# Side work placed between the pieces of a step, and a softmax handed out in stages, in a streaming attention layer

## The chip, the cores and the metric

The kernel runs on one core of one Trainium2 chip. The metric is the device time of one execution in microseconds. The profile is of one further execution on the same kind of core.

## What is computed

One layer of an encoder with two token mixers side by side, for one new stream of 2048 frames and for eight running streams of 16 frames with a past of 512. Cut to what matters here:

```
h = adaln(x, c);  qa, ka, va, za, qb, kb, vb, zb, ga, gb = split(h @ w_in)     # A and B, 512 wide each
# A, differential attention, 4 heads of 2 x 64
p = softmax(mask(qa . ka / 8));  oa = (p[first] - lam * p[second]) @ va
# B, stick-breaking attention, 8 heads of 64
log_a = log_sigmoid(z) + reverse_cumsum(log_sigmoid(-z)) - log_sigmoid(-z);  ob = exp(log_a) @ vb
# merge
y = (sigmoid(ga) * ((rms(oa) * silu(za)) @ w_branch_a) + sigmoid(gb) * ((ob * silu(zb)) @ w_branch_b)) @ w_out
```

The outputs are the normed streams and the new keys and values of both mixers.

## The kernel before

**Number format.** Every float32 operand of a large product is split into two float16 halves, a high and a low one, and a product is three matmuls. A split needs a power of two as its scale, and that comes from the sum of the squares of the operand. So each weight and each cached key or value is loaded (SyncE's queue), squared and summed on ScalarE (`sum_squares`, L282 in the profile), its sum is spread over the partitions by a small matmul (`total`, L221), and it is then split (`split`: the high half on ScalarE, L300, or on GpSimd, L302, the low half on VectorE, L305).

**Units and steps.** The main part of the kernel goes through eight units; even ones are a head of A, odd ones two heads of B. A unit has 17 steps: the tile of the sampled streams (`t == NT`, no scores here) and 16 tiles of 128 frames. A step of tile `t` computes the scores of that tile against all earlier keys in chunks of 512 (`scores`, L660 and L661, the mask L664), and takes some pieces of the projections, which run about five steps ahead on a line of their own (L446; the gate's, in B units, L522; the transposes L535 and L539).

**A's softmax.** The chunk's scores are copied out of their bank by VectorE with a running maximum (L576). After a tile's last chunk `softmax_pair` takes the maximum (L607), four exponentials on ScalarE for a tile of two segments (L124), the sums (L617 to L620), a join of the two softmaxes for each segment (L624), and then `turn`: the split into halves (L300, L305) and a transposing DMA into `wt` (L598).

**B's weights.** ScalarE takes two sigmoids of a chunk (L124), VectorE scans one of them straight out of the bank (L637), GpSimd multiplies (L643), and `turn` splits (L590, L591) and transposes.

**The products with the values.** `turn` puts the matmuls of a segment (L717 to L719 in A, L721 and L722 in B) on the list `due`, to be given out when `spent`, a count of the microseconds of TensorE's work that the text has given out, has grown by `PV_LAG`. `give` runs the pieces of a step in order, adds their cost to `spent`, and gives out what is due.

**Side work.** While unit u is at work, `prepare_unit(u + 1)` makes a list of pieces: loads of the next unit's weights with the squares one piece behind, the scale (`bounds`), the splittings (`cut`, `gate_cut`). Two further lists are `spare` (loads and squares of the last weights and of the cached values, L878) and `cached` (cached keys: load, square, then splitting and storing, L898 to L901). At the beginning of each step the loop takes some pieces off these lists and runs them, before the step's scores and projections:

```
for fn in back[: -(-len(back) // max(1, (W_READY if u else W_READY + 2) - t % NT))]:
    back.pop(0)()
```

**Order.** The program text gives each instruction a place; from it a scheduler with a model of the chip sets the order on each engine when the kernel is built. An instruction whose inputs the model takes as ready may be put ahead of others that stand before it in the text. `act` is a helper that chains ScalarE's table functions, so that these keep the order of the text; `sum_squares` does not use it. Raw buffers come from the list `free` and go back to it, so how early a load can be issued depends on the buffers. The bank tags are `mm` (2), `s` (3, the scores), `t` (1) and `o` (2).

**The end.** After the units, a last part multiplies with the branch weights and the output weights, and does the sampled streams' attention beside it (from about 1830 us on). The first part (to about 143 us) makes `h`.

Of the kernel before, what the change touches and what calls it, by code (L numbers as in the profile page):

```python
# [4 lines left out]


# [14 lines left out]
AF = mybir.ActivationFunctionType  # L21
# [4 lines left out]
P = 128  # L26
# [12 lines left out]
SEG = 8  # L39
PV_LAG = 30.0  # L40
PIECE, CHUNK, PV_A, PV_B = 0.44, 0.22, 0.17, 0.085
# [73 lines left out]
def layer_kernel(ctx: ExitStack, tc: tile.TileContext, a: dict):  # L115
# [160 lines left out]

    def sum_squares(src, n, dst, width=1024, scale=1.0):

        for i in range(0, n, width):
            junk = tiny.tile([P, width], F16, tag="junk", name="junk", bufs=1)  # L280
            w = min(width, n - i)
            S.activation(out=junk[:, 0:w], in_=src[:, i : i + w], func=AF.Square, scale=scale,  # L282
                         accum_out=dst[:, i // width : i // width + 1])

# [32 lines left out]
    def prepare_unit(u, keep=None):  # L317
# [30 lines left out]

# [234 lines left out]
    def turn(job, seg, scale=None):  # L583
# [15 lines left out]
        if job["t"] < NT:  # L599
            cost = (PV_A, PV_B)[job["U"]["kind"]]  # L600
            due.extend((spent[0] + PV_LAG, cost, fn) for fn in pv(job, seg))

    def softmax_pair(job):

        segs = job["segs"]
        nm = tiny.tile([P, 2], F32, tag="nm", name="nm")
        V.tensor_reduce(out=nm, in_=job["mx"][:, :, 0 : job["nch"]], axis=AX.X, op=ALU.max, negate=True)  # L607
        l = tiny.tile([P, 2, 2], F32, tag="l", name="l")
        for i, seg in enumerate(segs):
            nk = (seg["hi"] - seg["lo"]) * P  # L610
            for c in range(2):
                w = seg[("p", "n")[c]][:, 0:nk]
                act(out=w, in_=w, func=AF.Exp, bias=nm[:, c : c + 1], accum_out=l[:, c, i : i + 1])
        r = tiny.tile([P, 3], F32, tag="r", name="r")
        sums = l[:, :, 0]
        if len(segs) > 1:
            V.tensor_tensor(out=sums, in0=l[:, :, 0], in1=l[:, :, 1], op=ALU.add)  # L617
        V.reciprocal(out=r[:, 0:2], in_=sums)
        V.scalar_tensor_tensor(out=r[:, 2:3], in0=sums[:, 0:1], scalar=r[:, 1:2], in1=nlam, op0=ALU.mult, op1=ALU.mult)
        V.tensor_tensor(out=r[:, 0:1], in0=r[:, 0:1], in1=ls[:, 0:1], op=ALU.mult)  # L620
        for seg in segs:
            nk = (seg["hi"] - seg["lo"]) * P
            p, n = seg["p"][:, 0:nk], seg["n"][:, 0:nk]
            V.scalar_tensor_tensor(out=p, in0=n, scalar=r[:, 2:3], in1=p, op0=ALU.mult, op1=ALU.add)  # L624
            turn(job, seg, r[:, 0:1])

# [96 lines left out]

    due, spent = [], [0.0]

# [17 lines left out]
    def give(order, costs):  # L743

        for i, weight, fn in order:
            fn()
            spent[0] += weight * costs[i]
            while due and due[0][0] <= spent[0]:
                _, cost, product = due.pop(0)
                product()  # L750
                spent[0] += cost
# [109 lines left out]
    def norms():  # L861
# [124 lines left out]
    with tc.tile_pool(name="p0", bufs=1) as p0:  # L986
# [156 lines left out]
        interleave(normed(0))  # L1143
        for fn in early[0:5]:
            fn()
# [57 lines left out]
        interleave(modulated(4))  # L1203
        interleave([(1.0, fn) for fn in early[5:]], modulated(0), normed(1))
        free.extend(first_x)
# [119 lines left out]
    for n in range(len(steps) + 2):  # L1325
        made, qk = [], []
        if n < len(steps):
# [17 lines left out]
        if at[0] == len(line) and not pieces and not spare and not cached:  # L1345
# [4 lines left out]
            if n == len(steps) + 1:  # L1350
                pieces += [(PV_B / PIECE, fn) for _, _, fn in due]
                due.clear()
        give(interleaved(pieces, qk), (PIECE, CHUNK))
    c01.close()
# [158 lines left out]
```

## Time and profile before

| | us |
|---|---|
| median of three runs | 2300.79 |
| lowest, highest | 2296.86, 2304.49 |
| the profiled execution | 2304.59 |
| its span, first to last instruction | 2302.8 |
| mean granted TensorE clock | 0.969 |

The page of the profile gives each engine's busy time and share, and the costliest groups of instructions. The views by stretch give the busy time of each engine in a window of the span. In the lists of waits, a line "PE ps_s L660 <- DVE sc_n L637: 33.7, 38, 2.8" says that TensorE's matmuls of line 660 stood idle for 33.7 us in 38 waits, the longest 2.8, until an instruction of line 637 on VectorE was done. Names such as `sc_n` are the program's tiles: `sc_p` and `sc_n` hold scores, `wt` the transposed weights, `ps_...` are banks, `junk` is where the squares are thrown away, `wa` and `wb` are the buffers of the list `free`.

### The profile page before, as it was taken

The page shows a single profiled execution, that of the slowest core. Times are in us where ns is not written, and L with a number is a line of the kernel's source. Part 1 is how long each engine was busy: PE and PEld are TensorE (multiplying, and loading weights), DVE is VectorE, ACT ScalarE, POOL GpSimd, SP SyncE. Part 2 cuts the span into 40 slices and gives each one's busy share as a digit, 9 for nine tenths or more (in the row PEclk, how much of TensorE's full clock was granted, in tenths as well). Part 3 has the DMA queues.
Part 4 walks back from the last instruction along what each step waited for, and adds up shares of the span by engine and source line. Part 5 has one row for each costly group of instructions (what it writes and reads, how often), then busy time and mean ns, then how long its engine had stood idle before and what let it go on. Part 6 is the DMA issues. An engine that isn't in the chain of part 4 may idle for free. (4 is left out here: it accounts for less than half of the span.)

```text
span 2302.8 us, 41756 instructions
## 1 busy us (share of the span) xinstructions
PE 2098.3 (91%) x14752; PEld 1130.4 (49%) x14752; DVE 1724.1 (75%) x3795; ACT 1622.1 (70%) x3228; POOL 697.6 (30%) x610
## 2 busy tenths in 40 slices
PE   5999998988999999889998988999998688999998
PEld 3655554544555445455554544555454344444443
DVE  4668776779875877998676769976778877777663
ACT  4978776878876776887677788866677666566551
POOL 1232033456311433743033346401334311111211
PEclk8999999999999999999999999999998898999999
DMA  9778778888895898789779699774777899889431
GB/s 328 267 240 213 159 169 213 179 197 188 197 235 143 225 211 196 169 177 266 162 193 229 149 223 197 179 171 120 158 157 158 177 276 248 219 218 239 140 107 47
DMA packets 805827, 445.30 MB, mean 193 GB/s; under 512 B 537354, under 2 KB 744506, under 8 KB 805104
## 3 DMA queue, kind: packets, MB, share of 16 engines
q1 hardware_dynamic: 804668, 442.24, 78.3%
q8 instruction: 115, 1.88, 0.3%
q14 instruction: 96, 0.79, 0.1%
q10 hardware_dynamic: 948, 0.39, 0.1%
HBM read 228.82 MB, written 86.02 MB: 137 GB/s over the span
## 5 line engine op out<-in xcount | busy, mean ns | idle before, releaser
L643 POOL TENSOR_TENSOR sc_p<-sc_p,sc_n 128x127 f32<-128x127 f32 (+7 forms) x192 | 314.5, 1640 | 744.7 <-DVE sc_n L637 505.3
L446 PEld LDWEIGHTS <-hs 128*128 128x128 f16 x3120 | 293.7, 99 | 312.6 <-issue 7.9
L446 PE MATMUL ps_mm<-wb,hs 128*128 128x512 f16 x1734 | 433.8, 382 | 0.0
L446 PE MATMUL ps_mm<-wa,hs 128*128 128x512 f16 x1386 | 338.9, 380 | 1.9 <-DVE v L305 1.9
L637 DVE TENSOR_TENSOR_SCAN sc_n<-ps_s,sc_n,zero_t 128x512 f32<-128x512 f32 x192 | 245.6, 1279 | 67.3 <-ACT ps_s L124 62.8
L660 PE MATMUL ps_s<-k,qst 128*128 128x512 f16 (+3 forms) x640 | 225.4, 353 | 61.5 <-DVE sc_n L637 45.7
L522 PEld LDWEIGHTS <-hs 128*128 128x128 f16 x1632 | 156.3, 99 | 188.5 <-DVE qst L550 12.2
L591 DVE TENSOR_TENSOR sc_n<-sc_p,sc_n 128x128 f16<-128x128 f32 (+7 forms) x192 | 213.4, 1116 | 41.0 <-ACT sc_n L590 40.4
L124 ACT ACTIVATE sc_p<-ps_s,usc 128x512 f32<-128x512 f32 (+3 forms) x320 | 203.9, 637 | 41.1 <-PE ps_s L661 23.9
L661 PE MATMUL ps_s<-k,qst 128*128 128x512 f16 (+3 forms) x640 | 226.1, 354 | 0.0
L522 PE MATMUL ps_t<-wb,hs 128*128 128x512 f16 x918 | 218.8, 379 | 1.9 <-DVE qst L550 1.9
L124 ACT ACTIVATE ps_s<-ps_s,usc 128x512 f32<-128x512 f32 (+3 forms) x328 | 199.1, 607 | 0.0
L590 ACT CAST sc_n<-sc_p 128x128 f16<-128x128 f32 (+7 forms) x192 | 154.5, 808 | 62.7 <-POOL sc_p L643 62.0
L1427 PE MATMUL ps_o<-wo,wa 128*128 128x512 f16 x816 | 184.7, 382 | 0.7 <-ACT wa L1240 0.7
L522 PE MATMUL ps_t<-wa,hs 128*128 128x512 f16 x714 | 172.9, 384 | 8.1 <-DVE qst L550 4.7
L721 PE MATMUL ps_o<-v,wt 128*128 128x128 f16 x1088 | 132.4, 225 | 25.3 <-DMA wt<-sc_n 25.2
L576 DVE TENSOR_SCALAR_CACHE_REDUCE sc_p<-ps_s,usc 128x512 f32<-128x512 f32 (+3 forms) x160 | 106.2, 663 | 43.8 <-PE ps_s L661 28.4
L487 POOL TENSOR_TENSOR rot<-pr,rope 128x256 f32<-128x256 f32 x68 | 60.5, 889 | 245.9 <-ACT pr L460 202.8
L721 PEld LDWEIGHTS <-wt 128*128 128x128 f16 x1088 | 102.0, 102 | 55.0 <-DMA wt<-sc_n 31.8
L637 DVE TENSOR_TENSOR_SCAN sc_n<-ps_s,zero_t 128x128 f32<-128x128 f32 (+3 forms) x128 | 104.2, 814 | 32.0 <-ACT ps_s L124 31.3
L1427 PEld LDWEIGHTS <-wa 128*128 128x128 f16 x816 | 78.6, 98 | 95.3 <-issue 2.6
L722 PE MATMUL ps_o<-v,wt 128*128 128x64 f16 x1088 | 123.7, 197 | 0.0
(369 smaller groups left out, 4520.9 us busy)
## 6 DMA issues: line engine op xcount, KB each, us to landing
hs<-hT_d SPq DMA_DIRECT2D x130, 512.0 KB, 4.1
g_d<-gt SPq DMA_DIRECT2D x68, 256.0 KB, 5.3
wb<-g_d SPq DMA_DIRECT2D x34, 512.0 KB, 4.7
out_dram<-pr SPq DMA_DIRECT2D x204, 64.0 KB, 2.0
wa<-in_w_in_dram SPq DMA_DIRECT2D x34, 256.0 KB, 4.7
o_d<-o SPq DMA_DIRECT2D x136, 64.0 KB, 2.8
hs<-o_d SPq DMA_DIRECT2D x17, 512.0 KB, 7.1
out_dram<-x SPq DMA_DIRECT2D x17, 512.0 KB, 2.8
```

Source lines behind the costliest of these rows:

```text
L124: i = S.activation(**kw)
L446: T.matmul(box["p"], box["h"][:, hi, k, :], U["w"][k][:, wi, :], start=(n == 0), stop=(n == 3 * KT - 1))
L522: T.matmul(box["g"][:, 0:gw], box["h"][:, hi, k, :], U["wg"][k // per][:, k % per, wi, :], start=(j == 0), stop=(j == 3 * KT - 1))
L590: S.copy(out=hi, in_=src)
L591: V.tensor_tensor(out=lo, in0=src, in1=hi, op=ALU.subtract)
L637: V.tensor_tensor_scan(out=dst[:, lo : lo + n][:, ::-1], data0=src[:, 0:n][:, ::-1], data1=zero_t[:, 0:1].to_broadcast([P, n]), initial=fi ...
L643: G.tensor_tensor(out=p[:, 0:m], in0=p[:, 0:m], in1=n[:, 1 : m + 1], op=ALU.mult)
L660: T.matmul(p[:, 0:n], qst[:, c, :], kk[:, c, 0:n], start=True, stop=False)
L661: T.matmul(p[:, 0:n], qst[:, 2 + c, :], kk[:, c, 0:n], start=False, stop=not diag)
L721: T.matmul(po[:, c * P : (c + 1) * P], wt[:, wj, :], vt[:, c, :, :], start=first, stop=False)
L722: T.matmul(po[:, c * P : c * P + 64], wt[:, nb + wj, :], vt[:, c, 0, :], start=False, stop=last)
L1427: T.matmul(po, st["y"][:, yi * 8 + k, :], wo[j * 4 + k // 2][:, wi, k % 2, :], start=(n == 0), stop=(n == 3 * KT - 1))
```

## The change

1. `sum_squares` gets `keep`. With it, the square is pinned behind the instruction that stands before it in the text on ScalarE. It is set for the preparation of units 1 to 7, for `spare` and for `cached`.
2. In a preparation, a square stands two pieces behind its load, where it stood one behind. So each list of loads has one piece more, and the first stage runs six early pieces of unit 0 instead of five.
3. The pieces of `back`, `spare` and `cached`, and unit 7's branch weight, are collected in `side` and interleaved with the step's projections and chunks, at no cost in `spent`.
4. `softmax_pair` no longer issues everything at once. It puts stages on the list `due`, by work given out since the tile's last chunk: the exponentials at 1.0, the sums at 3.0 plus two for each full segment (`n_all` is the tile's length in segments of eight blocks), the join of segment i at that plus i, and its `turn` 1.5 later. The sampled tile's is still issued at once.
5. `PV_LAG` is 27 instead of 30; it counts from `turn`. The list `due` is now kept in order of due time.

```diff
-PV_LAG = 30.0
+PV_LAG = 27.0
+TURN_LAG = 1.5
+EXP_LAG = 1.0
+SUM_LAG = 2.0
...
-    def sum_squares(src, n, dst, width=1024, scale=1.0):
+    def sum_squares(src, n, dst, width=1024, scale=1.0, keep=False):
...
+            x = S.activation(out=junk[:, 0:w], in_=src[:, i : i + w], func=AF.Square, scale=scale,
+                             accum_out=dst[:, i // width : i // width + 1])
+            if keep:
+                tc.keep_in_program_order(x)
...
-            sum_squares(raw[name, k], 1024, U[name + "acc"][:, i : i + 1])
+            sum_squares(raw[name, k], 1024, U[name + "acc"][:, i : i + 1], keep=u > 0)
...
-                if i > 0:
-                    norm(name, ks[i - 1], i - 1)
-            return [lambda i=i: piece(i) for i in range(len(ks) + 1)]
+                if i > 1:
+                    norm(name, ks[i - 2], i - 2)
+            return [lambda i=i: piece(i) for i in range(len(ks) + 2)]
...
-            due.extend((spent[0] + PV_LAG, cost, fn) for fn in pv(job, seg))
+            for fn in pv(job, seg):
+                later_on(PV_LAG, fn, cost)
...
+        stages = [(EXP_LAG, lambda i=i, c=c: powers(i, c)) for i in range(len(segs)) for c in range(2)]
+        stages.append((EXP_LAG + SUM_LAG + 2.0 * n_all, sums))
+        for i, seg in enumerate(segs):
+            at = EXP_LAG + SUM_LAG + 2.0 * n_all + i
+            stages += [(at, lambda seg=seg: joined(seg)), (at + TURN_LAG, lambda seg=seg: turn(job, seg, r[:, 0:1]))]
+        for lag, fn in stages:
+            if job["t"] == NT:
+                fn()
+            else:
+                later_on(lag, fn)
...
+    def later_on(lag, fn, cost=0.0):
+
+        spent[1] += 1
+        bisect.insort(due, (spent[0] + lag, spent[1], cost, fn))
...
-                sum_squares(st, 1024, dst, scale=scale)
+                sum_squares(st, 1024, dst, scale=scale, keep=True)
...
-            sum_squares(fetched[0][0], 1024, acc)
+            sum_squares(fetched[0][0], 1024, acc, keep=True)
...
-        for fn in early[0:5]:
+        for fn in early[0:6]:
...
             if u == 7 and not back and not spare and not cached and len(branch_weights) > 1:
-                branch_weight()
+                side.append((1.0, branch_weight))
             for fn in back[: -(-len(back) // max(1, (W_READY if u else W_READY + 2) - t % NT))]:
-                back.pop(0)()
+                side.append((1.0, back.pop(0)))
...
-                        todo.pop(0)()
+                        side.append((1.0, todo.pop(0)))
...
-        give(interleaved(pieces, qk), (PIECE, CHUNK))
+        give(interleaved(pieces, qk, side), (PIECE, CHUNK, 0.0))
```

`powers`, `sums` and `joined` hold the same instructions as before, in functions of their own.

More of the change, by code (lines that the diff above doesn't have):

```diff
@@ L7 @@
+import bisect
 import math
@@ L281, in sum_squares @@
             w = min(width, n - i)
-            S.activation(out=junk[:, 0:w], in_=src[:, i : i + w], func=AF.Square, scale=scale,
-                         accum_out=dst[:, i // width : i // width + 1])
+            x = S.activation(out=junk[:, 0:w], in_=src[:, i : i + w], func=AF.Square, scale=scale,
+                             accum_out=dst[:, i // width : i // width + 1])
+            if keep:
+                tc.keep_in_program_order(x)
     def add_up(acc, n):
@@ L608, in softmax_pair, with powers, sums, joined @@
         l = tiny.tile([P, 2, 2], F32, tag="l", name="l")
[L609 to L613, printed above, removed]
-        r = tiny.tile([P, 3], F32, tag="r", name="r")
[L615 to L621, printed above, removed]
+        r = tiny.tile([P, 3], F32, tag="r", name="r")
+        n_all = sum(seg["hi"] - seg["lo"] for seg in segs) / SEG
+        def powers(i, c):
+            seg = segs[i]
+            w = seg[("p", "n")[c]][:, 0 : (seg["hi"] - seg["lo"]) * P]
+            act(out=w, in_=w, func=AF.Exp, bias=nm[:, c : c + 1], accum_out=l[:, c, i : i + 1])
+        def sums():
+            sums = l[:, :, 0]
+            if len(segs) > 1:
+                V.tensor_tensor(out=sums, in0=l[:, :, 0], in1=l[:, :, 1], op=ALU.add)
+            V.reciprocal(out=r[:, 0:2], in_=sums)
+            V.scalar_tensor_tensor(out=r[:, 2:3], in0=sums[:, 0:1], scalar=r[:, 1:2], in1=nlam, op0=ALU.mult, op1=ALU.mult)
+            V.tensor_tensor(out=r[:, 0:1], in0=r[:, 0:1], in1=ls[:, 0:1], op=ALU.mult)
+        def joined(seg):
             nk = (seg["hi"] - seg["lo"]) * P
@@ L722, in pv_block @@
             T.matmul(po[:, c * P : c * P + 64], wt[:, nb + wj, :], vt[:, c, 0, :], start=False, stop=last)
-    due, spent = [], [0.0]
+    due, spent = [], [0.0, 0]
+    def later_on(lag, fn, cost=0.0):
+        spent[1] += 1
+        bisect.insort(due, (spent[0] + lag, spent[1], cost, fn))
     def pv(job, seg):
@@ L748, in give @@
             while due and due[0][0] <= spent[0]:
-                _, cost, product = due.pop(0)
+                _, _, cost, product = due.pop(0)
                 product()
@@ L1203, in layer_kernel @@
         interleave(modulated(4))
-        interleave([(1.0, fn) for fn in early[5:]], modulated(0), normed(1))
+        interleave([(1.0, fn) for fn in early[6:]], modulated(0), normed(1))
         free.extend(first_x)
@@ L1325, in layer_kernel @@
     for n in range(len(steps) + 2):
-        made, qk = [], []
+        made, qk, side = [], [], []
         if n < len(steps):
@@ L1350, in layer_kernel @@
             if n == len(steps) + 1:
-                pieces += [(PV_B / PIECE, fn) for _, _, fn in due]
+                while due and due[0][2] == 0.0:
+                    due.pop(0)[3]()
+                pieces += [(PV_B / PIECE, fn) for _, _, _, fn in due]
                 due.clear()
-        give(interleaved(pieces, qk), (PIECE, CHUNK))
+        give(interleaved(pieces, qk, side), (PIECE, CHUNK, 0.0))
+    for _, _, _, fn in due:
+        fn()
     c01.close()
```

1 line of the change is left out of this document (removed).

## The prediction

> **What bounds the kernel now.** I read the page first, then the busy time of each engine by stretch, then TensorE's own waits, then who waits in the line that sums squares, and last a stretch of the timeline.
>
> ```profile
> PE 2098.3 (91%) x14752; PEld 1130.4 (49%) x14752; DVE 1724.1 (75%) x3795; ACT 1622.1 (70%) x3228; POOL 697.6 (30%) x610
> ```
>
> TensorE is busy for 91% of the span and no other engine for more than 75%, so the time is TensorE's work plus its idle time. The next view gives, for stretches cut where the score work changes kind, the length and then the busy microseconds of PE, PEld, DVE, ACT and POOL, and after them the granted clock. In order they are the units 0 (A), 1 (B), 2 (A), 3 (B), 4 (A), 5 (B), 6 (A), and 7 (B) up to where its projections run out.
>
> ```profile
> 143.00:298.00 155.00, 149.79 (x1059) 83.33 (x1057) 124.72 (x351) 123.15 (x279) 27.64 (x29) 0.99 0.78 197
> 298.00:548.00 250.00, 231.66 (x1595) 122.76 (x1593) 194.26 (x322) 193.34 (x399) 113.12 (x89) 0.98 0.84 193
> 548.00:728.00 180.00, 167.69 (x1155) 93.30 (x1155) 139.33 (x384) 134.27 (x302) 40.68 (x45) 0.97 0.83 191
> 728.00:979.00 251.00, 230.88 (x1643) 124.90 (x1641) 198.24 (x333) 194.13 (x399) 112.50 (x91) 0.99 0.87 200
> 979.00:1157.00 178.00, 166.65 (x1164) 93.03 (x1163) 140.38 (x388) 135.42 (x304) 40.68 (x45) 0.98 0.83 196
> 1157.00:1415.00 258.00, 234.66 (x1635) 125.61 (x1633) 195.84 (x328) 196.89 (x407) 113.69 (x93) 0.97 0.88 202
> 1415.00:1586.00 171.00, 162.04 (x1152) 89.25 (x1152) 138.67 (x380) 122.22 (x279) 41.65 (x42) 1.00 0.69 162
> 1586.00:1755.00 169.00, 165.51 (x1161) 88.76 (x1160) 134.57 (x226) 121.29 (x256) 63.40 (x50) 1.00 0.70 158
> ```
>
> Unit 7 is the control that this kernel carries in itself. It does the same score work as units 1, 3 and 5, with VectorE as busy (134.57 of 169, 80%, against 198.24 of 251, 79%), but it has next to no side work, and TensorE is busy for 97.9% of it, against 92.7, 92.0 and 91.0% in units 1, 3 and 5. So side work costs TensorE time where it stands now, and VectorE's load alone does not. At unit 7's share, units 1, 3 and 5 would last 236.6, 235.8 and 239.7 us, which is 46.9 less; at unit 0's share (96.6%), units 2, 4 and 6 would last 173.6, 172.5 and 167.7, 15.2 less. These 62 us bound what a better order of side work can give.
>
> What TensorE waits for between 143 and 1755 us (total, times, longest), and below it the same for unit 1 and for the control:
>
> ```profile
> PE ps_s L660 <- DVE sc_n L637: 33.7, 38, 2.8
> PE ps_o L717 <- DMA wt<-sc_n: 14.7, 10, 3.8
> PE ps_s L660 <- DVE sc_n L576: 9.1, 7, 3.3
> PE ps_o L721 <- DMA wt<-sc_n: 7.2, 6, 2.3
> ...
> PE ps_s L660 <- DVE sc_n L637: 9.9, 10, 2.8
> ...
> PE ps_s L660 <- DVE sc_n L637: 1.5, 1, 1.5
> ```
>
> The first row is a score matmul without a free bank, since the scan that empties the bank is late. Units 3 and 5 show the same 9.9 as unit 1; the control shows 1.5 in 169 us.
>
> Why the scan is late is seen at the line that sums squares, where ScalarE sits idle until a load lands:
>
> ```profile
> L282 ACT ACTIVATE junk<-wa x64: 1038/1057/1112, 250.4 to 1463.1; 128x1024 f16<-128x1024 f32 x64
> ...
>   DMA wa<-in_cache_a_k_dram: 14.4, 9
>   DMA wb<-in_w_in_dram: 14.2, 10
>   DMA wa<-in_w_in_dram: 13.0, 6
>   DMA wa<-in_cache_b_k_dram: 10.9, 7
>   DMA wb<-in_cache_b_k_dram: 7.2, 4
>   DMA wb<-in_cache_b_v_dram: 6.3, 2
>   DMA wa<-in_cache_a_v_dram: 6.0, 3
> ```
>
> These seven rows are 72.0 us of ScalarE standing still for squares in 41 waits. None of it is in the control, as the last of these squares starts at 1463.1. One of them in the timeline (start, length, engine and line; in brackets the idle time before and what ended it):
>
> ```profile
> 812.61 0.40 SPq L878 DMA_DIRECT2D wa<-in_cache_a_v_dram  x1
> ...
> 818.55 1.06 ACT L282 ACTIVATE junk<-wa 128x1024 f16<-128x1024 f32 x1 [3.93 <-DMA wa<-in_cache_a_v_dram]
> ...
> 819.99 0.35 DVE L305 SCALAR_TENSOR_TENSOR k<-ps_mm,usc,k 128x128 f16<-128x128 f32 x1 [3.50 <-ACT k L300]
> ...
> 822.53 0.22 PE L660 MATMUL ps_s<-k,qst 128*128 128x128 f16 x1 [1.21 <-DVE sc_n L637]
> ```
>
> The load was issued at 812.61. ScalarE reached its square 2.0 us later (818.55 less 3.93) and stood, with the key's split, the cast and the sigmoids queued behind it; VectorE then stood 3.50 and TensorE 1.21. In the program text that square is a whole step behind its load, so the schedule moved it up, to where it takes the load as landed.
>
> **The change, part by part.** *Squares in ScalarE's order.* The pin holds each square behind the instruction that the text puts before it on ScalarE, so it can no longer move up to its load, while the load can still be early. No instruction is added. In units 1, 3 and 5 the scan waits are 3 x 9.9 = 29.7; at the control's rate (1.5 in 169 us) 6.7 of them would stay in these 759 us. The difference is 23.0 us, which is 0.32 us of TensorE for each us of the 72.0. I take all 23.0, as the control has the same scans. Its ends are 0 (VectorE, at 79%, makes the scans late anyway) and the 46.9 above.
>
> *What the pin adds.* A square that does come up before its load now stands at a fixed place, and ScalarE's casts and sigmoids stand behind it. Where could that be? A unit's preparation begins in the short step of the sample tile, where three pieces fall close together and two pieces of lag are little. The load itself takes
>
> ```profile
> wa<-in_w_in_dram SPq DMA_DIRECT2D x34, 256.0 KB, 4.7
> ```
>
> so two squares in each of seven preparations could stand up to 4.7 us: 65.8 us of ScalarE, times 0.32, 21 us of TensorE. I take 1.5, since two buffers or more are free there and a load is issued when its buffer is free, not when its piece comes up. The other end is 0.
>
> *Side work over the step.* The loads, splittings and halvings keep their count. They come one by one between score chunks, where before they stood at the step's head and went first on GpSimd, VectorE and SyncE. On SyncE the loads are moved in between the transposing transfers of the weights; a load that gets behind one is late by a few us, which the square's lag covers, and if that cover is gone it is the 21 us just named. GpSimd is 45% busy in the B units and has the room. What smoother work is worth is inside the 23.0 already, because the control lacks both squares and splittings; I add nothing, with +-10 us for the range.
>
> *A's softmax in stages.* Of one tile these are the parts (the last three figures of each row before its idle time are count, busy us, mean ns):
>
> ```profile
> L624 DVE SCALAR_TENSOR_TENSOR sc_p<-sc_n,r,sc_p 128x1024 f32<-128x1024 f32 (+4 forms) x96 | 97.8, 1047 | 0.0
> L305 DVE SCALAR_TENSOR_TENSOR sc_n<-sc_p,r,sc_n 128x1024 f16<-128x1024 f32 (+4 forms) x96 | 97.4, 1034 | 3.2 <-ACT sc_n L300 2.8
> L124 ACT ACTIVATE sc_p<-sc_p,nm 128x1024 f32<-128x1024 f32 (+4 forms) x96 | 85.5, 891 | 15.1 <-DVE nm L607 15.1
> L300 ACT ACTIVATE sc_n<-sc_p,r 128x1024 f16<-128x1024 f32 (+4 forms) x96 | 83.9, 896 | 30.5 <-DVE sc_p L624 30.3
> ```
>
> A long tile (two segments) puts two joins and two splittings on VectorE, 2 x (1047 + 1034) ns = 4.2 us, all ahead of the next tile's evacuations. Given out in stages they stand behind those evacuations in the text. What can go is the third row of TensorE's waits, 9.1 us; I take half, 4.5, with 0 and 9.1 as its ends. The chain itself is four exponentials, the joins and a splitting, 4 x 0.89 + 2 x 1.05 + 0.90 + 1.03 = 7.6 us, so a turn can hardly leave earlier today than the 8.5 us of work at which the stages ask for it. A's products come up 31.75 to 36.5 us of work after the last chunk, where it was 30. The second row, 14.7 us, I leave as it is.
>
> *PV_LAG 27 in B.* A B product may come 3 us earlier behind its transfer. The fourth row has 6 waits; each could be 3 longer, 18 in all, or none. As 6 of 192 segments (2 heads, 24 a unit and head, 4 units) wait at all, I take 2.
>
> *A rule that speaks against the stages.* The table loads of ScalarE are
>
> ```profile
> L124 ACT ACT_TABLE_LOAD x15 | 19.2, 1283 | 0.2
> ```
>
> and an exponential that falls among the next unit's sigmoids would add two of them. This could happen at four borders between A and B: 4 x 2 x 1.283 = 10.3 us of ScalarE, 3.3 of TensorE. I take 0: exponentials fall due after 1.0 us of work, and the sample tile's step between two units gives out about three pieces of 0.44 and has no sigmoid. The Trainium skill (ScalarE: Activation LUTs, section Table sets: the hidden batching unit) says to do all calls of one table set before the next, and the same page counts a drain with each switch, some 2.66 us together; by that the border would cost an estimated 6.8 us of TensorE, and the rows here show no more than 1.283 each.
>
> *With one answer:* six early pieces for five in the first stage, the branch weights of unit 7, and the flush at the end move nothing that TensorE waits for: 0.
>
> **Sum.** -23.0 + 1.5 - 4.5 + 2 = -24.0 us. The profiled execution took 2304.6 us (its span is 2302.8), so it would come to 2280.6; the median of the runs shown is 2300.79, 3.8 lower, which gives 2277.
>
> **The rivals.** *All of the side work's cost goes* (chance 0.15). The B units reach the control's share and the A units unit 0's: 62 us, 2239. For it: VectorE is equally busy in the control. The clock would add to it: the B units stand at 0.98, 0.99 and 0.97, the control at 1.00. The Trainium skill (TensorE: Matmul & The Clock Gate, section HAM oscillation) says that it takes an idle stretch of about 3.4 us to lower the clock; the longest waits above are 3.8 and 3.3, so by that rule only the gaps themselves come back, and I count no clock. Against the rival: transposing transfers (21.9 us of waits) are untouched.
>
> *The stalls only move* (0.13). Pinned squares meet their loads in the short steps (the 21 us above), or VectorE makes the scans late whatever ScalarE does. Then 20 of the 24 are eaten, and the time is 2297 to 2301.
>
> *A's turns come too late* (0.17, slower). The stages hold the turn back to 8.5 or 9.5 us of work after the last chunk, and TensorE still takes the product as soon as the schedule believes the weights landed. Now 10 of 96 segments wait 14.7 us, 1.47 each. Twenty more waiting segments cost 29 us and outweigh the 24; if half of the 96 wait, 38 more, it is +56 - 24 = +32 us, 2333. For it: such waits reach 3.8 us, so the products are already asked for close behind the transfer. Against: the chain of 7.6 us, and the later place of the products.
>
> **How the numbers follow.** The forecast has 0.55, with a range of its own of 2255 to 2293 (46 to 8 us less: the pin's ends, thinned). My range is 2240 to 2312: it takes in nearly all of the first rival and all of the second, and leaves out most of the third and a sliver at the bottom. About 0.3%, 7 us, is what a measurement of this kernel can tell from no change; the runs shown lie 7.6 apart. Faster by more than that: the forecast and the first rival, 0.70; same 0.13; slower 0.17.
>
> **What would show it.** Right: ScalarE's waits for loads at the line of the squares fall from 72 to under 25 us; the scan waits of units 1, 3 and 5 fall from 29.7 towards 7; TensorE's share in them rises from 92% to 95 or more; the waits of L660 for the A evacuations halve. Wrong: waits for the weights' transfer in A above 40 us (third rival); ScalarE's load waits as long as now but in the sample tile's steps (second); more than 15 table loads; or load waits gone and the scan waits still there, which would mean that VectorE sets them.

## The result, and the profile after

The kernel became faster: 2274.18 us (median of six runs, 2265.63 to 2280.78) against 2300.89 (2291.51 to 2306.21), a ratio of 0.9886 with a 95% interval of 0.9857 to 0.9915. The profiled execution took 2280.78 us with a span of 2279.0 and a mean granted clock of 0.970; it is 23.8 us shorter than the profiled execution of before.

The page's line of busy time, after:

```profile
PE 2086.9 (92%) x14752; PEld 1122.3 (49%) x14752; DVE 1716.8 (75%) x3795; ACT 1617.6 (71%) x3228; POOL 701.4 (31%) x610
```

Every engine executes as many instructions as before, so only their order and their waits can have changed. Next, the view by stretch as in the prediction, units 0 to 7 (length, busy time of PE, PEld, DVE, ACT and POOL, then the granted clock):

```profile
141.00:315.00 174.00, 155.30 (x1031) 84.51 (x1030) 127.56 (x363) 125.93 (x285) 23.58 (x29) 0.95 0.70 176
315.00:550.00 235.00, 225.54 (x1618) 121.97 (x1617) 191.27 (x315) 188.04 (x390) 114.01 (x90) 0.99 0.89 202
550.00:725.00 175.00, 168.49 (x1223) 93.94 (x1222) 138.60 (x398) 137.87 (x314) 40.42 (x45) 1.00 0.81 202
725.00:965.00 240.00, 223.61 (x1584) 119.40 (x1582) 196.34 (x318) 188.52 (x387) 117.03 (x92) 0.99 0.92 206
965.00:1142.00 177.00, 170.39 (x1218) 94.72 (x1216) 139.78 (x399) 139.08 (x315) 41.13 (x45) 0.98 0.81 200
1142.00:1383.00 241.00, 224.77 (x1579) 119.75 (x1577) 197.03 (x321) 188.74 (x389) 118.59 (x92) 0.99 0.92 210
1383.00:1554.00 171.00, 163.72 (x1164) 89.83 (x1162) 136.03 (x382) 130.14 (x296) 38.72 (x43) 1.00 0.70 170
1554.00:1720.00 166.00, 158.84 (x1099) 84.80 (x1098) 128.54 (x217) 114.89 (x243) 57.45 (x49) 0.99 0.67 150
```

TensorE's share in units 1, 3 and 5 rose from 92.7, 92.0 and 91.0% to 96.0, 93.2 and 93.3% (225.54 of 235, and so on). Those units are 15, 11 and 17 us shorter than before, units 2 and 4 are 5 and 1 us shorter. Unit 0 is the loser: 19 us longer, its share down from 96.6 to 89.3%. Unit 7, the prediction's control, lost share as well, from 97.9 to 95.7%; its longest wait is one of 4.8 us for the transfer of `hs`.

TensorE's waits over these stretches (total, times, longest), after. The lines have moved: the scores' L660 is L681 here, the scan L637 is L658, the A evacuation L576 is L582, the products L717 and L721 are L738 and L742, the projection L446 is L452, the squares L282 are L286.

```profile
PE ps_o L738 <- DMA wt<-sc_n: 25.6, 13, 6.2
PE ps_s L681 <- DVE sc_n L658: 19.2, 18, 3.0
PE ps_mm L452 <- DMA hs<-hT_d: 13.4, 5, 4.8
PE ps_s L681 <- DVE csc L924: 7.3, 7, 1.8
PE ps_s L681 <- DVE sc_p L582: 3.9, 5, 2.5
PE ps_o L742 <- DMA wt<-sc_n: 3.4, 3, 1.4
...
PE ps_s L681 <- DVE sc_n L582: 2.4, 4, 1.5
```

Of before, these rows of the same list had not been shown:

```profile
PE ps_t L522 <- DVE qst L550: 6.5, 5, 3.0
PE ps_t L221 <- DVE qst L550: 6.0, 2, 3.5
PE ps_s L660 <- DVE sc_p L576: 4.7, 9, 1.3
PE ps_s L221 <- ACT junk L282: 4.2, 2, 2.6
PE ps_t L535 <- DVE k L305: 3.8, 6, 1.1
```

All rows of the list together are 101.5 us before and 86.9 after, 14.6 less. Grouped by what ended the wait, the balance is:

| ended by | before | after | change |
|---|---|---|---|
| B's scans (L637) | 35.3 | 22.2 | -13.1 |
| A's evacuations (L576) | 14.2 | 6.3 | -7.9 |
| the split of the queries (`qst`) | 12.5 | 3.3 | -9.2 |
| squares, key splits (`junk`, `k`) | 8.0 | 0.5 | -7.5 |
| the weights' transposing transfer (`wt`) | 21.9 | 29.0 | +7.1 |
| the transfer of `hs` for the projections | 0 | 13.4 | +13.4 |
| the cached keys' scale (`csc`) | 4.4 | 7.3 | +2.9 |
| the rest | 5.2 | 4.9 | -0.3 |

So 38 us of waits on VectorE and ScalarE went, and 23 us of waits came, 20 of them on transfers. The stretch of the eight units, from its first evacuation to its last projection, went from 1602.9 to 1578.6 us, 24.3 less, which is the whole difference. I divided it by going from the start of each matmul to the start of the next, and setting off first the matmul's length at full clock, then idle time, then what the half clock added. Both kernels have 1451 us of full-speed work; idle time went from 102 to 87, the half clock's part from 20 to 16, and 30 to 24 us is small change in between. The gain is 15 us of idle time, 4 of clock and 6 of small change.

The waits of units 1, 3 and 5 for the scan, and what is left of ScalarE's waits for loads at the squares:

```profile
PE ps_s L681 <- DVE sc_n L658: 7.0, 7, 3.0
...
PE ps_s L681 <- DVE sc_n L658: 5.6, 5, 2.9
...
PE ps_s L681 <- DVE sc_n L658: 6.7, 6, 2.9
```

```profile
  DMA wa<-in_cache_a_k_dram: 10.3, 6
  DMA wa<-in_cache_b_k_dram: 6.3, 5
```

The scan waits went from 29.7 to 19.3, the load waits from 72.0 to 16.6. What is left belongs to the cached keys; no weight and no cached value makes a square wait any more.

### The profile page after: what moved, and what is told of

It is laid out like the page before. It is cut to its first block, busy times and chain, and to the rows that moved or that the text cites. A ratio compares the mean times of both kernels' runs of the same rounds, so it can differ in the third digit from the quotient of the medians.

```text
span 2279.0 us, 41771 instructions
## 1 busy us (share of the span) xinstructions
PE 2086.9 (92%) x14752; PEld 1122.3 (49%) x14752; DVE 1716.8 (75%) x3795; ACT 1617.6 (71%) x3228; POOL 701.4 (31%) x610
## 5 line engine op out<-in xcount | busy, mean ns | idle before, releaser
L664 POOL TENSOR_TENSOR sc_p<-sc_p,sc_n 128x127 f32<-128x127 f32 (+7 forms) x192 | 319.2, 1664 | 701.7 <-DVE sc_n L658 529.6
L452 PEld LDWEIGHTS <-hs 128*128 128x128 f16 x3120 | 293.4, 99 | 332.4 <-DMA hs<-hT_d 15.5
L452 PE MATMUL ps_mm<-wa,hs 128*128 128x512 f16 x1590 | 389.8, 384 | 9.5 <-DMA hs<-hT_d 8.6
L452 PE MATMUL ps_mm<-wb,hs 128*128 128x512 f16 x1530 | 376.9, 381 | 5.8 <-DMA hs<-hT_d 4.8
L528 PE MATMUL ps_t<-wb,hs 128*128 128x512 f16 x1224 | 290.7, 380 | 1.3 <-DVE qst L556 1.0
L658 DVE TENSOR_TENSOR_SCAN sc_n<-ps_s,sc_n,zero_t 128x512 f32<-128x512 f32 x192 | 245.4, 1278 | 48.9 <-ACT ps_s L128 44.2
L681 PE MATMUL ps_s<-k,qst 128*128 128x512 f16 (+3 forms) x640 | 226.0, 354 | 46.3 <-DVE sc_n L658 31.3
L1457 PE MATMUL ps_o<-wo,wb 128*128 128x512 f16 x816 | 182.9, 379 | 0.7 <-ACT wb L1266 0.7
L742 PE MATMUL ps_o<-v,wt 128*128 128x128 f16 x1088 | 131.4, 224 | 18.8 <-DMA wt<-sc_n 18.7
L582 DVE TENSOR_SCALAR_CACHE_REDUCE sc_n<-ps_s,usc 128x512 f32<-128x512 f32 (+3 forms) x160 | 106.4, 665 | 46.5 <-PE ps_s L685 30.8
L1457 PEld LDWEIGHTS <-wb 128*128 128x128 f16 x816 | 78.1, 98 | 94.5 <-issue 1.2
L738 PE MATMUL ps_o<-v,wt 128*128 128x128 f16 x544 | 100.4, 222 | 25.8 <-DMA wt<-sc_n 25.6
L658 DVE TENSOR_TENSOR_SCAN sc_n<-ps_s,zero_t 128x128 f32<-128x128 f32 (+3 forms) x128 | 104.0, 813 | 25.5 <-ACT ps_s L128 24.9
L742 PEld LDWEIGHTS <-wt 128*128 128x128 f16 x1088 | 101.1, 101 | 44.2 <-DMA wt<-sc_n 24.8
L582 DVE TENSOR_SCALAR_CACHE_REDUCE sc_p<-ps_s,usc 128x512 f32<-128x512 f32 (+3 forms) x160 | 106.2, 664 | 21.3 <-PE ps_s L682 14.2
```

What stands on the lines that cost most here:

```text
L452: T.matmul(box["p"], box["h"][:, hi, k, :], U["w"][k][:, wi, :], start=(n == 0), stop=(n == 3 * KT - 1))
L528: T.matmul(box["g"][:, 0:gw], box["h"][:, hi, k, :], U["wg"][k // per][:, k % per, wi, :], start=(j == 0), stop=(j == 3 * KT - 1))
L582: V.tensor_scalar(out=dst[:, lo : lo + n], in0=p[:, 0:n], scalar1=sc_pos, scalar2=None, op0=ALU.mult, op1=ALU.max, accum_out=job["mx"][:, ...
L658: V.tensor_tensor_scan(out=dst[:, lo : lo + n][:, ::-1], data0=src[:, 0:n][:, ::-1], data1=zero_t[:, 0:1].to_broadcast([P, n]), initial=fi ...
L664: G.tensor_tensor(out=p[:, 0:m], in0=p[:, 0:m], in1=n[:, 1 : m + 1], op=ALU.mult)
L681: T.matmul(p[:, 0:n], qst[:, c, :], kk[:, c, 0:n], start=True, stop=False)
```

## The experiments

Two theories were to be told apart. One is the prediction's: squares that stand at their loads hold up ScalarE, and each us of that costs TensorE about a third, whatever else is done. The rival says that the parts work only together, or that the time depends on the order as a whole and the waits just move. In the following, "load waits" are those of ScalarE at the squares between 130 and 1800 us (before 78.0, after 16.6), "scan waits" those of all score matmuls for B's scans in the same stretch (before 45.7, after 31.3). Ratios are against the kernel before on the same chip.

**The pin alone.** To the kernel before:

```diff
+            if keep:
+                tc.keep_in_program_order(x)
...
+            sum_squares(raw[name, k], 1024, U[name + "acc"][:, i : i + 1], keep=u > 0)
```

and `keep=True` for `spare` and `cached`; the lag stays one piece.

> The kernel before with the squares of units 1 to 7, of the spare and of the cached list pinned in ScalarE's order and nothing else changed. Theory (the pin carries the gain): ScalarE's waits for loads at the squares fall from 72 to under 30 us, the scan waits of units 1, 3 and 5 from 29.7 to about 12, and the time by 15 to 23 us, to about 2282. Rival (spreading the side work carries it): the load waits fall, the scan waits stay above 25, and the time stays within 7 us of 2301. Rival (the stages carry it): the same.

2299.67 us, 0.9983 [0.9967, 0.9999]. The load waits fell to 27.4 and the scan waits to 31.8, and yet the kernel gained 4 us, not 23. In the order of the two traces, the pin does what it says: in the kernel before, a square stands a median of 30 of ScalarE's 2636 other instructions earlier than in this one (128 squares, up to 176 earlier). TensorE's waits in the units show where the rest went:

```profile
PE ps_s L662 <- DVE sc_n L639: 20.5, 25, 2.8
PE ps_o L719 <- DMA wt<-sc_n: 14.9, 10, 3.6
PE ps_mm L448 <- DMA hs<-hT_d: 12.1, 6, 5.0
PE ps_o L723 <- DMA wt<-sc_n: 10.9, 6, 4.0
PE ps_s L662 <- DVE sc_p L578: 10.1, 9, 4.5
```

The scan's row is 13.2 lower than before (33.7). The third row is new, the fourth is up by 3.7 and the last by 5.4: 21.2 came back, through the transfers of `hs` and `wt` and through A's evacuations into `sc_p`. Smaller rows fell, and all rows together are 97 us against 101.5. The time is the one that the rivals gave, but the scan waits, 20.5 us in all units, are under the 25 that they asked for in three.

**The pin and the lag of two pieces,** without spreading and stages.

```diff
-                if i > 0:
-                    norm(name, ks[i - 1], i - 1)
+                if i > 1:
+                    norm(name, ks[i - 2], i - 2)
```

> The kernel before with the pin and two pieces of lag, nothing spread and no stages. The pin alone gave 2300 with 27 us of load waits left. Theory (the pin needs the spreading or the stages): 2293 to 2300. Rival (the pin only lacked the second piece of lag): load waits under 20 us and 2285 or less.

2318.76 us, 1.0053 [1.0035, 1.0071]. The load waits fell to 14.9, as low as in the whole change, the scan waits to 32.8, and the kernel became slower. ScalarE's other waits for transfers rose from 13.1 to 29.6. Neither theory had asked for a slower kernel. The stalls that the prediction was about are gone here and the time is not better: one us of load waits is not a third of a us of time.

**The stages alone,** in a list kept by due time, with `PV_LAG` 27, on the kernel before.

> The kernel before with A's softmax in stages, the ordered due list and PV_LAG 27, and nothing else. Theory: 4.5 us from A's evacuations less 2 for the lag, so 2 to 5 us faster, within what can be told from no change. Rival (the stages carry the gain): 15 us faster or more. Rival (turns too late): A's waits for the weights' transfer rise from 14.7 to 25 us or more, and the time is 5 to 10 us longer.

2316.2 us, 1.0053 [1.0038, 1.0068], with 75.7 us of load waits. TensorE's waits:

```profile
PE ps_s L679 <- DVE sc_n L656: 43.6, 30, 4.3
PE ps_o L736 <- DMA wt<-sc_n: 22.1, 11, 5.3
```

The scan waits rose by 9.9 against the row of before, and A's weights cost 7.4 more. The last rival comes nearest, with 12 us lost and 22.1 us of waits for the 25 that it asked for, but the larger rise is that of the scans, which it did not name.

**The spreading alone.** On the kernel before, `back.pop(0)()` and the two other calls become `side.append((1.0, back.pop(0)))`, and `give` gets `interleaved(pieces, qk, side)`.

> The kernel before with the side work interleaved with the step's pieces, no pin, one piece of lag, no stages. Theory: ScalarE's load waits stay at 60 to 80 us since nothing holds the squares, and the time stays within 7 us of 2301. Rival (spreading carries the gain): 15 us faster or more, with the scan waits of units 1, 3 and 5 near 15 us.

2327.67 us, 1.0104 [1.0083, 1.0125], with 66.6 us of load waits. TensorE's waits:

```profile
PE ps_s L660 <- DVE sc_n L637: 29.9, 29, 4.1
PE ps_o L717 <- DMA wt<-sc_n: 24.8, 15, 3.6
PE ps_mm L446 <- DMA hs<-hT_d: 9.8, 7, 2.8
```

The scans wait 3.8 less than before, A's weights 10.1 more, and the loads of `hs` are late, as in the pin alone. The load waits came as the theory said; the loss of 24 us neither had forecast. That the loads which spreading moves between the transposing transfers cause it fits these two rows, but no run shows it by itself.

**The whole change without the pin:**

```diff
-            if keep:
-                tc.keep_in_program_order(x)
```

> The changed kernel without the pin; two pieces of lag, spreading and stages kept. Theory: load waits come back to 60 to 80 us, scan waits of units 1, 3 and 5 to 25 or more, and 15 to 20 of the 27 us are lost: about 2290. Rival (spreading or stages): under 7 us are lost, so under 2281, whatever the load waits do.

2332.83 us, 1.0119 [1.0096, 1.0142]. Taking this line out turns 27 us of gain into 29 us of loss, where the theory had asked for 15 to 20 us. The squares stand a median of 18 of the 2636 instructions earlier than with the pin (up to 146), and wait for all kinds of loads again, 76.1 us in all; the largest rows at the line of the squares:

```profile
  DMA wa<-in_cache_a_k_dram: 18.1, 9
  DMA wa<-in_cache_b_k_dram: 16.7, 6
```

TensorE's waits:

```profile
PE ps_s L679 <- DVE sc_n L656: 34.6, 27, 2.7
PE ps_o L736 <- DMA wt<-sc_n: 14.4, 10, 4.5
PE ps_s L679 <- DVE sc_p L580: 10.7, 10, 2.1
PE ps_s L679 <- DVE sc_n L580: 9.7, 8, 2.2
```

Against the rows of after the scan is 15.4 up and A's evacuations 14.1, while A's weights are 11.2 down. By the count from matmul to matmul the stretch of the units is 50 us longer than after: 33 of idle time, 12 of half clock, 4 of small change.

**The whole change, A's softmax at once.** `softmax_pair` runs its parts one after the other, as before the change; `PV_LAG` stays 27, so A's products are also 3 us of work earlier than in the kernel before.

> The changed kernel with A's softmax issued at once again (PV_LAG 27, pin, two pieces of lag and spreading kept). Theory from the first four runs (each part alone gains 4 or loses 12 and 24, so the pin pays by holding squares still once the others have made the rest of ScalarE's text later): the pin and the spreading are enough, about 2280, less than 10 us lost. Rival (the stages earn their place once the pin is there): 2290 or more, with scores waiting for A's evacuations at 12 us or more.

2298.1 us, 0.9965 [0.9946, 0.9983]. The rival's time came, and its wait did not: the scores wait 5.6 us for A's evacuations, where it asked for 12 or more and the kernel with the stages has 6.3.

```profile
PE ps_s L678 <- DVE sc_n L582: 3.6, 6, 1.6
...
PE ps_s L678 <- DVE sc_p L582: 2.0, 3, 1.3
```

So with the pin and the spreading, A's evacuations cost little with the stages and without them. Grouped as in the table of the result, what is higher without the stages are the waits for B's scans (27.5 against 22.2), for the split of the queries (9.5 against 3.4) and for B's weights (8.1 against 3.4).

**The whole change, side work at the step's head.** The three `side.append` become calls again.

> The changed kernel with the side work at the step's head again (pin, two pieces of lag, stages and PV_LAG 27 kept). Theory: the spreading is what keeps a pinned square from meeting its load, so ScalarE's load waits rise from 17 to 25 us or more and the time to 2290 or more. Rival (the pin with two pieces of lag is enough): load waits stay under 20 us and the time under 2282.

2301.33 us, 0.9971 [0.9952, 0.9990]. The load waits are 32.8 us, so the theory came out on both counts. ScalarE's waits for transfers, in the units:

```profile
ACT wa L306 <- DMA keys_bk<-wa: 18.4, 4, 5.5
ACT junk L286 <- DMA wa<-in_cache_a_k_dram: 17.4, 6, 7.1
```

The first row was 4.3 us before and is 2.9 in the whole change: at the step's head, by the text, the splitting of a cached key comes right behind the storing of the key before it. All of ScalarE's waits for transfers apart from the squares' are 44.9 us, against 9.7 in the whole change.

With these the parts can be put together. Each ratio is the kernel's against before:

| | neither | spreading | stages | both |
|---|---|---|---|---|
| without the pin | 1 | 1.0104 | 1.0053 | 1.0119 |
| with the pin and the lag | 1.0053 | 0.9965 | 0.9971 | 0.9886 |

(In the first row only "both" has the lag of two pieces; in "spreading", second row, and "both" A's products have `PV_LAG` 27.) Without the pin, spreading and stages each lose; with it, each gains 0.8 to 0.9%, and the two together 1.7%. The pin by itself, with the lag of one piece, is worth 0.2%; in their company, 2.3%.

**How much an order alone is worth.** Two sizes without a cost of their own: `PV_LAG` back to 30, and the exponentials half a us later.

```diff
-PV_LAG = 27.0
+PV_LAG = 30.0
```

> The changed kernel with PV_LAG 30 instead of 27. Theory: 2 us or so either way, 2270 to 2280, and it shows how far a small shift of the text moves the time by the order alone. Rival (the lag matters): 2285 or more, or 2265 or less, with the waits for the weights' transfer in A, 25.6, moved by 8 us or more.

2291.95 us, 0.9921 [0.9898, 0.9944]. Both signs of the rival came: the time, and A's waits for the weights, 14.3 us lower than 25.6:

```profile
PE ps_o L738 <- DMA wt<-sc_n: 11.3, 9, 4.1
```

Yet the kernel is slower and not faster. By the count from matmul to matmul the stretch of the units is 16 us longer than in the whole change, and only some 5 of these are idle time: the half clock takes 28 us where it took 16. The intervals of the two kernels overlap a little (0.9898 to 0.9944, and 0.9857 to 0.9915), so a difference is likely but not sure.

```diff
-EXP_LAG = 1.0
+EXP_LAG = 1.5
```

> The changed kernel with the first stage of A's softmax due after 1.5 us of work instead of 1.0, and the later stages 0.5 later with it: a shift that no theory gives a price, as a measure of what a new order alone does. If orders are worth little: 2270 to 2280. If an order alone is worth 8 us or more either way, as the 2292 with the lag of 30 let one think: outside that.

2298.28 us, 0.9967 [0.9951, 0.9983]. The scan waits are as in the whole change (31.5), the waits for A's weights are lower (16.3 against 25.6), and others are higher: B's weights (9.4 against 3.4), A's evacuations (9.3 against 6.3), the split of the queries (15.0 against 3.4), and ScalarE's load waits (28.0 against 16.6). The profiled execution is 17 us longer, 11 of them in the stretch of the units and 6 outside it. No single row explains the loss; many small waits have changed places. So differences of up to 0.8% between two kernels of this family say little about the part that was changed: the two parts' 0.8 to 0.9% in the table are of that size, and stand on the pattern only. The pin's 2.3% is three times as large. And the eight kernels that have the pin and at least one of the other two parts lie between 0.9864 and 0.9971, while the three without it lie between 1.0053 and 1.0119.

**Squares right behind their loads.** In the whole change, the pinned square comes in the same piece as its load, in the preparations, in `spare` and in `cached`.

```diff
-                if i > 1:
-                    norm(name, ks[i - 2], i - 2)
+                    norm(name, ks[i], i)
...
```

In `cached` the splitting of a key moves up by one piece with its square.

> The changed kernel with each pinned square right behind its load in the text, in the same piece (unit 0's too, which are not pinned). Theory (the pin pays because it keeps squares away from their loads): ScalarE's load waits rise from 17 to over 100 us, and at 0.3 us of TensorE for each the time rises by 25 us or more over 2274, to 2300 or more. Rival (the loads are early anyway, and the pin pays by the place it gives the square among ScalarE's other work): load waits under 40 us, and the time under 2285.

2291.72 us, 0.9944 [0.9929, 0.9960]; load waits 38.8, which is 22 more than in the whole change. With a load that takes 4.7 us and over a hundred such squares I had looked for more than 100. Most loads have landed when ScalarE comes to their squares; 18 squares wait. The rival's load waits came, under 40, but its time (under 2285) did not: the kernel is 0.6% slower than the whole change. These 22 us of stalls are not what costs it. By the count from matmul to matmul the stretch of the units is 13 us longer than in the whole change, and TensorE's idle time is under 2 us of that (89 against 87); the half clock takes 27 us where it took 16. So the distance from the load explains little of what the pin does. That the pin's effect lies in the place which it gives the square among ScalarE's other work is what remains; no run here shows it by itself.

**The new waits for `hs`.** `H_AT` is the piece of a step at which the next `hs` is loaded; 0 is the first.

```diff
-H_AT = 2
+H_AT = 0
```

> The changed kernel with the next step's input half fetched at the first piece of a step instead of the third. Theory (the projections' waits for that load, 13.4 us in 5 waits and none before, are a wait that took the place of others): they fall under 5 us and the time by 5 to 10 us, to about 2267. Rival (they are hidden by what comes next): within 5 us of 2274.

2280.65 us, 0.9899 [0.9882, 0.9915], the same as the whole change within the intervals. TensorE's waits:

```profile
PE ps_o L742 <- DMA wt<-sc_n: 11.0, 6, 2.9
...
PE ps_mm L452 <- DMA hs<-hT_d: 3.8, 2, 3.2
```

The waits for `hs` fell from 13.4 to 3.8, and those for B's weights rose from 3.4 to 11.0. Both transfers are issued from the same queue, and most of what the one gained (9.6) the other lost (7.6). The theory's time, 2267, did not come.

**Unit 0.** Its new idle time is this row of after, from 141 to 315 us:

```profile
PE ps_o L738 <- DMA wt<-sc_n: 12.1, 3, 6.2
```

During unit 0 unit 1 is prepared. The experiment leaves that preparation unpinned:

```diff
-            sum_squares(raw[name, k], 1024, U[name + "acc"][:, i : i + 1], keep=u > 0)
+            sum_squares(raw[name, k], 1024, U[name + "acc"][:, i : i + 1], keep=u > 1)
```

> The changed kernel with the pin of the preparations from unit 2 on only, so that unit 1's preparation, which runs beside unit 0, is free as it was before. Theory: unit 0 had under 2 us of load waits before and lost 13.5 us of idle TensorE time with the change; without the pin there its idle time falls from 18.7 towards 8 and the time to 2264 to 2270. Rival (what unit 0 lost unit 1 gained, 21.7 to 9.5, since the work only moved across their border): no change, 2270 to 2280.

2273.96 us, 0.9864 [0.9844, 0.9884]. It is the fastest kernel that ran, but its interval and that of the whole change (0.9857 to 0.9915) overlap, so the time is the rival's. In unit 0 TensorE's share is 92.2%, its idle time 12.9 us (18.7 in the whole change, 8 by the theory), and the row is smaller:

```profile
143.00:307.00 164.00, 151.13 (x1026) 81.87 (x1025) 127.95 (x355) 122.47 (x278) 24.96 (x28) 0.99 0.76 187
...
PE ps_o L738 <- DMA wt<-sc_n: 8.5, 5, 3.2
```

## Why the prediction was right, and where it was not

The time (2277 for 2274.18, and -24.0 for the -23.8 of the profiled execution) came out, and so did the sign. Its terms did not all do so: the sum is right because misses on both sides cancel, and that is luck. Of its signs, the load waits came (16.6, under 25) and the evacuations (13.8 to 6.3, more than half); the scan waits stopped at 19.3 on the way to 7, and TensorE's share reached 95% in one of the three units.

- **The pin, -23.0: the step that failed.** It took the squares' stalls as a cost of its own, 0.32 us of TensorE for each us. The stalls did go (72.0 to 16.6, forecast under 25). But the scan waits of units 1, 3 and 5 fell by 10.4, not 23.0, and alone the pin made 4 us, with the lag it made the kernel 12 us slower, while in company it decides some 54 us (1.0119 less 0.9886, of 2301). No single price per us of stall gives all of these. The control misled, in two ways. It lacks all parts of the side work at once, so it says nothing of the squares alone. And it is not the same score work, as the prediction had it: units 1, 3 and 5 have 80 scans each, and unit 7 has only 56 of its 80 before 1755 us, where the prediction's stretch ends. The other 24 are of its longest tiles, and there, without any side work but also without projections to fill the time, the scores wait longer than in any of the three units:

```profile
1755.00:1830.00 75.00, 43.95 (x367) 26.55 (x366) 63.11 (x93) 50.81 (x82) 36.47 (x22) 0.75 0.75 157
...
PE ps_s L660 <- DVE sc_n L637: 12.0, 11, 1.8
```

  In units 1, 3 and 5, too, the late tiles are where the waits are: 20.2 of the 29.7 us fall into the last quarter of the units (6.6, 7.0 and 6.6), and after the change 13.9 of the 19.3. So the rate of 1.5 in 169 us was too low for what would stay, and it was not shown that side work, and not VectorE, makes the scans late.
- **Spreading, "nothing added": too low, as far as an order alone lets one say.** With the pin it is worth 0.85% (0.9971 less 0.9886, 20 us), and without it it costs 1.0%. What can be named of it are ScalarE's waits for transfers apart from the squares', the storing of keys above all, 44.9 to 9.7 us.
- **Stages, -4.5: the wait named is not the one that they change.** The waits for A's evacuations fell from 14.2 to 6.3, but without the stages they are 5.6, so the stages are not what took them away; with the stages and no pin they are 20.4. The whole part, again with the pin, is 0.8% (0.9965 less 0.9886), and it shows in other rows: scans, the split of the queries, B's weights.
- **A's weights, "as it is": wrong.** 14.7 became 25.6, and 12.1 of that is in unit 0. The third rival's mechanism is there, but in 13 waits for 96 segments, not in thirty or more, so it took 11 us and not 29. That the stages hold the turns back is not shown to be the reason: without them these waits are 22.4, with them and a lag of 30 11.3, and 11.1 with the squares right behind their loads.
- **`PV_LAG` 27, +2: wrong sign, small.** B's waits for weights went from 7.2 to 3.4, but with 30 they are 4.0, so the lag did not do it. Whether 27 helps is not shown, since 30 (0.9921) is within what an order alone does.
- **Pinned squares that meet their loads, +1.5: the place was wrong.** No square of a weight waits, so the short step of the sample tile costs nothing there. All 16.6 us are in cached keys, which the prediction had not named; by its own price they would be 5.3 us, but that price does not hold.
- **Missed altogether:** the waits for `hs`, +13.4. I had the loads move between the transposing transfers of the same queue, but did not list what else that queue brings. Missed as well was the other side: the splits of queries and keys and the squares, 16.7 us of waits less.
- **Table loads:** 15, as forecast, so the rule that spoke against the stages did not come into play:

```profile
L128 ACT ACT_TABLE_LOAD x15 | 19.2, 1283 | 0.2
```

- **The clock, not counted:** 4 of the 24 us. Before, the half clock cost 20 us in the units, though almost all waits there were shorter than 3.4 us (the longest in the list 3.8). In the trace of before, eleven of the twelve stretches at half clock in the units (3.4 us each, two of them 6.8) begin inside one wait of 1.9 to 3.8 us or within 1.3 us of its end, and nine of these waits are shorter than 3.4; ahead of the twelfth stand four short waits, 1.7 us together. Two further waits of 2.3 us have no half clock behind them. The wait for a scan that begins at 395.0 us is of 2.2 us, and the clock behind it (the third figure from the end) is 0.50:

```profile
395.00:397.40 2.40, 0.24 (x2) 0.12 (x2) 1.54 (x2) 2.40 (x6) 0.00 (x0) 1.00 1.30 220
397.40:400.80 3.40, 3.40 (x14) 1.48 (x13) 1.75 (x3) 2.82 (x6) 1.23 (x1) 0.50 0.94 332
```

  After, all eight stretches begin so, at waits of 2.3 to 6.2 us, and three waits of 1.9 to 2.9 us have none. The Trainium skill (TensorE: Matmul & The Clock Gate, section HAM oscillation) asks for an idle stretch of about 3.4 us, and by it I counted no clock; here single waits of 1.9 us and more were mostly enough. The Trainium skill (TensorE: Matmul & The Clock Gate, section A second HAM failure mode: psum-queue depth-cycling) tells of a kernel in which many micro-idles between groups of matmuls were enough. Of the twenty stretches here only the one behind four short waits looks like that.

Of the rivals, the second (stalls only move) is what the pin alone shows, 2299.67 for the 2297 to 2301 given. In the whole change half of it is true: 38 us of waits went and 23 came.

Open is why spreading and stages lose without the pin. An unpinned square goes ahead of later work wherever the builder's model takes its load as landed, and spreading gives it more such places: that fits the displaced squares of the kernel without the pin and its load waits, but the waits that rise there are several, and no run separates them. Open is also which part of the 1.1% belongs to this one order. Whether the remaining 16.6 us at the cached keys would go with one more raw buffer was not tried.

## What to carry to other kernels

Price a stall by what stands behind it, not by a rate: removing 50 us of stalls of a side engine gained 4 us alone and decided some 54 in company, and the waits that grew in their place were in good part on transfers of the one queue. Where an order is made by a scheduler with a model, pin the instructions that the model places too early first, and only then try to spread other work; and before believing a difference of half a per cent, change a neutral size and see what the order alone does (here up to 0.8%). Count what a control holds before using its rate: this one had 56 of 80 scans and left out the longest tiles. When a control lacks several parts at once, it can bound their sum at best, and says nothing on any one of them. And when a time changes and the waits do not, look at the granted clock: two of the kernels here lost 11 to 12 us more to the half clock than the whole change, with only 2 to 5 us more idle time.

## What the runs showed of the hardware

Loads were mostly done earlier than I had thought: with no piece between load and square, the squares waited 38.8 us in all, about 0.3 us for each of some 120 in the units, though a load of a weight took a median of 4.7 us from issue to landing in the kernel before. And one transfer that is issued late costs TensorE nearly its whole way: the `hs` load issued at 1337.81 us in the profile after ended a wait of 4.09 us at 1342.05. Both lines are of its timeline (start, length, engine and line, in brackets the idle time before).

```profile
1337.81 0.43 SPq L429 DMA_DIRECT2D hs<-hT_d  x1
...
1342.05 2.57 PE L452 MATMUL ps_mm<-wa,hs 128*128 128x512 f16 x6 [4.09 <-DMA hs<-hT_d]
```
